# Where the normalised keys of a hybrid RWKV-7/GLA layer lie, and when their row sums are taken

## The chip, the cores and the metric

The kernel runs on one core of a Trainium2 chip. The metric is device time in microseconds (us) of one execution. A core has five engines with a queue of instructions each: TensorE (PE in the profile, with its weight loads as PEld), VectorE (DVE), ScalarE (ACT), GpSimd (POOL), and SyncE (SP), which here only issues DMAs. Each engine takes its queue strictly in order; between engines, instructions wait on semaphores.

## The reference

One layer of a decoder, for 1024 prompt tokens and 8 sequences of 4 sample tokens. What matters here is the RWKV-7 half of the mixing step (8 heads of 64 columns, so 512 columns each for r, k and v):

```python
xs = pa + (prev - pa) * mu                       # token shift of the projected columns
r, k, v, w_lo, a_lo, g_lo = split_cols(xs, [...])
decay = jnp.exp(-jnp.exp(w)); a = jax.nn.sigmoid(a0 + a_lo @ a_up)
kk = heads(k * k_k)
kk = kk * lax.rsqrt(jnp.maximum(jnp.sum(kk * kk, -1, keepdims=True), 1e-24))
k = k * (1.0 + (a - 1.0) * k_a)
# per token:  S = S*decay + (S @ -kk) (kk*a)^T + v k^T ;  o = S @ r
```

The second half of the mixing step is gated linear attention (GLA). Then come an output projection, a layer norm, a ConvGLU feed-forward of width 2816 and a second layer norm. The feed-forward is not touched.

## The kernel before

Everything is float32. Large products are taken in three passes over a high and a low part (`wh`, `wl` of the weights, `xh`, `xl` of the tokens), all accumulated in one PSUM bank.

The mixing step goes in two halves of tokens (H0: 512 prompt and 32 sample tokens, in two blocks of 272; H1: 512 prompt tokens, one block) and, within a half, in four pairs of heads. So there are eight pairs, numbered 0 to 7. `rwkv_prep` (L847) does one pair: with `shifted` (L766) it projects k, then r, then v, 128 columns each. One block of a projection is 24 matmuls into a bank of the PSUM pool `g`, which has two banks; then ACT evicts it and DVE adds the shifted rows, reading the same bank, so a bank comes free only after DVE's reads. `pair_rsqrt` (L288) normalises the keys: PE sums the squares `sq` over each head (`t<-sel,sq`, into the PSUM pool `t`, also two banks), DVE takes the inverse root by Newton steps on the small tile `rst` (L276 to L286), ACT spreads it over `sq` (L290), and PE transposes `sq` (`t<-ident,sq`, L75). From that DVE forms `kk` (L898), then `ar` (L910), POOL forms `ba` = kk times a (L908), and DVE forms `bk` from `ba` (L920). `post` (L938) needs `ar` and `bk` for its products `t<-ar,bk`.

Tiles with one tag share one place in SBUF and hold it one after the other. In `p2` the tag `e1` holds `sw`, then `sq`, then `ba`; the tag `e4` holds `kk` and then `v`. So the first write of `v` (ACT, L778) waits until the last reader of `kk` is done.

Five chains (chunk recurrence, inverse, tail and so on) and three streams (RWKV projections, GLA projections, output projection) are woven by a planner, `weave` (L187), which counts PE's time and steps a thread at each `yield`. The framework under it then sets the order in each engine's queue from its own estimate of when operands are ready, so the queues differ from the order of the text: orders shown below are those of the queues.

Of the kernel before, what the change touches and what calls it, by code (L numbers as in the profile page):

```python
# [9 lines left out]
F32 = mybir.dt.float32  # L10
# [7 lines left out]
P = 128  # L18
# [25 lines left out]
def step_kernel(  # L44
# [73 lines left out]
    def col(j):  # L118
        return vec[:, j:j + 1]
# [13 lines left out]
    p2 = cx.enter_context(tc.tile_pool(name="p2", bufs=1))  # L133
# [78 lines left out]
    def s1(shape, name, i):  # L212
        return rr_.tile(shape, F32, name=name, tag=f"s{i}")
# [6 lines left out]
    def win_tile(c0, m=P, raws=(None, None)):  # L220
        out = []
        for raw, k0 in zip(raws, (0, 4)):
            raw = raw or win_load(c0, k0, m)
            wh = px.tile([P, 4, m], F32R, name="wh", tag="wh", bufs=3)
            act.copy(wh, raw)  # L225
            wl = px.tile([P, 4, m], F32R, name="wl", tag="wl", bufs=3)
            pool.tensor_tensor(wl, raw, f(wh), ALU.subtract)  # L227
            out += [(wh[:, j, :], wl[:, j, :]) for j in range(4)]
        return out

    def gemm(ps, ws, s, e, m=P):
        for k in range(KT):
            wh, wl = ws[k]
            o = ps[:m, 0:e - s]
            pe.matmul(o, wh, xh[:, k, s:e], start=k == 0, stop=False)
            yield 0
            pe.matmul(o, wh, xl[:, k, s:e], start=False, stop=False)
            yield 0
            pe.matmul(o, wl, xh[:, k, s:e], start=False, stop=k == KT - 1)
            yield 0  # L240

    def gtile():
        return pg.tile([P, 512], F32, name="g", tag="g")
# [7 lines left out]
    def s3(ap):  # L251
        return ap.rearrange("p (b t) -> p b t", t=NS)
# [10 lines left out]
    def rows_rsqrt(cols, n, v0, v1, op0, op1):  # L263
        ps = ttile()
        for j in range((n + P - 1) // P):
            w = min(P, n - P * j)
            for sq, sel, c in cols:
                m = sel.shape[1]
                pe.matmul(ps[0:w, 32 * (2 * j + c):32 * (2 * j + c + m)], sq[:, P * j:P * j + w],
                          sel.unsqueeze(2).to_broadcast([P, m, 32]), start=True, stop=True)  # L270
        ps = ps.rearrange("p (x r) -> p x r", r=32)[:, :, 0]
        st = p1.tile([P, 3, 10], F32, name="rst", tag="rst", bufs=2)
        a, y, t = [st[:, i, 0:10 if n > 512 else 8] for i in range(3)]
        if n > 512:
            pool.memset(a[:, 8:10], 1.0)
            dve.tensor_scalar(a[0:32, 8:10], ps[0:32, 8:10], v0, v1, op0, op1)  # L276
        dve.tensor_scalar(a[:, 0:8], ps[:, 0:8], v0, v1, op0, op1)
        newton(a, y, t)
        return y
# [8 lines left out]
    def pair_rsqrt(sq, n, *ops):  # L288
        y = rows_rsqrt([(sq, sel2, 0)], n, *ops)
        act.copy(sq[:, 0:512].rearrange("p (a c) -> p a c", c=64), y[:, 0:8].unsqueeze(2).to_broadcast([P, 8, 64]))  # L290
        return y

    def pair_spread(ye):
        ps = ttile()
        for j in range(4):
            pe.transpose(ps[:, j * P:(j + 1) * P], ye[:, j * P:(j + 1) * P], ident)
        return ps
# [468 lines left out]
    def shifted(H, c0, xs, ws=None):  # L766
        ft = c0 // P
        ws = ws or win_tile(c0)
        mu, halo_ = col(V_MU + ft), halo[:, ft:ft + 1]

        def add_prev(out, prev):
            dve.scalar_tensor_tensor(out, prev, mu, out, ALU.mult, ALU.add)
        for s, e in H.blocks:
            ps = gtile()
            yield from gemm(ps, ws, s, e)
            ep = min(e, 512)
            m = ep - s
            act.activation(xs[:, s:e], ps[:, 0:e - s], AF.Identity, scale=omu[:, ft:ft + 1])  # L778
            add_prev(xs[:, s + 1:ep], ps[:, 0:m - 1])
            add_prev(xs[:, s:s + 1], halo_)  # L780
            dve.tensor_copy(halo_ if H.base + ep < NP else nsh[:, ft, 0:1], ps[:, m - 1:m])
            if e > 512:
                pv, xv = s3(ps[:, 512 - s:544 - s]), s3(xs[:, 512:544])
                add_prev(xv[:, :, 1:], pv[:, :, 0:NS - 1])
                add_prev(xv[:, :, 0], sst[:, ft, :])
                dve.tensor_copy(nsh[:, ft, 1:9], pv[:, :, NS - 1])
# [9 lines left out]
    def take(gen, n):  # L796
        for _, item in zip(range(n), gen):
            yield item
# [48 lines left out]
    def rwkv_prep(Q):  # L847
        H, p = Q.H, Q.p
        n, sam = H.n, H.sam
        pcs = Q.pcs = rr_.tile([P, 8], F32, name="pcs", tag="pcs", bufs=3)  # L850
        pc0 = p * P
        cs = slice(pc0, pc0 + P)
        sw = p2.tile([P, 544], F32, name="sw", tag="e1")
        aa = s1([P, 544], "aa", 0)
        k = s1([P, 544], "k", 2)
        main = shifted(H, 512 + pc0, k)
# [28 lines left out]
        sq = p2.tile([P, 544], F32, name="sq", tag="e1")  # L885
        act.activation(sq[:, 0:n], k[:, 0:n], AF.Square, scale=col(V_KK + p))
        rr = s1([P, 544], "r", 3)
        yield from shifted(H, pc0, rr)
        y = pair_rsqrt(sq, n, 1e-24, 0.0, ALU.max, ALU.add)
        if Q.i >= 2:  # L890
            yield ("wait", f"C{Q.i - 2}")
        Q.E = rr_.tile([P, 8, 2, 2, CH], F32, name="E", tag="E", bufs=2)
# [1 line left out]
        Q.bkT = rr_.tile([P, 8, P], F32, name="bkT", tag="bkT", bufs=2)  # L894
        Q.ar = ars[Q.i % 2]
        Q.bon = rr_.tile([P, 512], F32, name="bon", tag="bon", bufs=2)
        kk = p2.tile([P, 544], F32, name="kk", tag="e4")
        dve.scalar_tensor_tensor(kk[:, 0:512], k[:, 0:512], col(V_KK + p), pair_spread(sq), ALU.mult, ALU.mult)  # L898
        if sam:
            ps = ttile()  # L900
# [3 lines left out]
            dve.scalar_tensor_tensor(kk[:, 512:544], k[:, 512:544], col(V_KK + p), ps[:, 0:32], ALU.mult, ALU.mult)  # L904
        arp = Q.ar
        bk = rr_.tile([P, 8, 2, CH], F32, name="bk", tag="bk")
        ba = p2.tile([P, 544], F32, name="ba", tag="e1")
        pool.tensor_tensor(ba[:, 0:n], kk[:, 0:n], aa[:, 0:n], ALU.mult)  # L908
        for h in range(2):
            dve.scalar_tensor_tensor(arp[own[h], :, 0, 1 - h, :], c3(kk)[own[h]], -1.0, pp[own[h], :, 0:CH],  # L910
# [264 lines left out]
    for hf, (base, n, blocks) in enumerate(HALVES):  # L1175
        H = Half()
# [95 lines left out]
    def stream_r():  # L1272
        for hf, H in enumerate(Hs):
            if hf:
                yield ("wait", "G0")
                yield from load_x(H)
                yield ("done", "X1")
            yield ("wait", "lock")
            yield from half_start(H, *([] if hf else [ws0]))
            yield ("free", "lock")  # L1280
            if hf == 0:
                constants()
                yield ("done", "X0")
            for Q in Qs[4 * hf:4 * hf + 4]:
                yield ("prio", R_PRIO[Q.i])
                yield ("wait", "lock")
                yield from rwkv_prep(Q)
                yield ("free", "lock")
# [468 lines left out]
```

## Time and profile before

| what | value |
|---|---|
| three runs | 1653.04, 1675.87, 1679.36 us |
| median | 1675.87 us |
| profiled execution, its own time | 1657.51 us |
| its span, first to last instruction | 1655.8 us |
| busy: PE, DVE, ACT, POOL | 95%, 57%, 32%, 22% |
| mean granted PE clock | 0.974 |

Idle time of PE is small as a share, and it lies almost all in the mixing step, which is the first 690 us. The runs differ among themselves by 1.6%. A row of the timeline gives start, duration, engine, line, operation, tile written, tiles read, count and, in brackets, how long the engine stood idle before it and what ended that.

### The profile page before, as it was taken

The numbers are of one execution on the slowest core, as the hardware profiler recorded it, in microseconds if no ns is written. First come the engines' busy times: TensorE is split into PE (matmuls) and PEld (weight loads), VectorE is DVE, ScalarE is ACT, GpSimd is POOL, SyncE is SP. The second block draws the span as 40 slices with busy tenths as digits, with TensorE's granted clock in tenths as the row PEclk, the third lists the DMA queues.
The fourth block names the chain that finished last, engine by engine and source line by source line (L and its number), as shares of the span: only waits on it lengthen the run. The fifth ranks groups of instructions, "written<-read, shape, count | busy, mean of one in ns | idle before, by whom it ended". The sixth has DMA issues, their size and how long they took to land.

```text
span 1655.8 us, 28781 instructions
## 1 busy us (share of the span) xinstructions
PE 1570.6 (95%) x11728; PEld 1324.3 (80%) x11728; DVE 945.6 (57%) x2083; ACT 529.4 (32%) x986; POOL 358.7 (22%) x583
## 2 busy tenths in 40 slices
PE   7899889889999999998999999999999999999997
PEld 6788777766676667666878898898988889888996
DVE  4566567676787767536774444544445443454348
ACT  4453443435444435344223131221202212121222
POOL 5434424323444343331000000000000000000005
PEclk9999998989999989999999999999999999999999
DMA  4122122131211013232313020210202112021102
GB/s 140 47 65 65 39 65 71 34 85 33 59 39 46 27 46 103 79 105 87 100 43 102 26 64 27 64 52 27 64 25 65 45 34 64 14 77 43 48 27 106
DMA packets 138572, 97.36 MB, mean 59 GB/s; under 512 B 15963, under 2 KB 127003, under 8 KB 138440
## 3 DMA queue, kind: packets, MB, share of 16 engines
q1 hardware_dynamic: 138440, 95.52, 19.5%
q8 instruction: 92, 1.51, 0.4%
q14 instruction: 40, 0.33, 0.1%
HBM read 84.36 MB, written 11.15 MB: 58 GB/s over the span
## 4 chain that ended last, share of the span: by engine, by line
PE 60%; DVE 5%; issue 2%; ACT 1%; POOL 1%; DMA 1%; DVEq 0%; POOLq 0%; ACTq 0%
PE g L71 26%; PE t L71 18%; PE dn L71 13%; PE t L75 1%; PE opso L71 1%; PE sps L71 1%; PE opsog L71 1%; DVE st L1485 0%; PE up L71 0%; DVE rst L285 0%; DVE yt L1665 0%; DVE ya L1642 0%; DVE tm L327 0%; DVE yt L1666 0%; PE rp L71 0%
## 5 line engine op out<-in xcount | busy, mean ns | idle before, releaser
L71 PE MATMUL g<-xh,wh 128*128 128x272 f32 (+1 forms) x624 | 221.3, 355 | 9.5 <-DVE sg L1094 3.5
L71 PE MATMUL g<-xh,wl 128*128 128x272 f32 (+1 forms) x624 | 215.2, 345 | 3.2 <-POOL wl L227 3.2
L71 PE MATMUL g<-xl,wh 128*128 128x272 f32 (+1 forms) x624 | 216.2, 347 | 0.0
L1458 DVE TENSOR_TENSOR wlu<-wraw,whu 128x1024 fp32r<-128x1024 f32 x45 | 55.1, 1224 | 229.2 <-ACT whu L1453 220.2
L227 POOL TENSOR_TENSOR wl<-wraw,wh 128x512 fp32r<-128x512 f32 x104 | 136.3, 1313 | 168.8 <-ACT wh L225 154.2
L1607 POOL COPY ncv<-gp 128x2 f32<-128x2 f32 x22 | 20.6, 936 | 610.1 <-ACT gp L1599 610.1
L71 PEld LDWEIGHTS g<-xh,wh 128*128 128x128 f32 x624 | 122.0, 196 | 22.6 <-issue 7.0
L71 PEld LDWEIGHTS g<-xh,wl 128*128 128x128 f32 x624 | 122.2, 196 | 11.4 <-POOL wl L227 3.7
L71 PE MATMUL g<-xb,whu 128*128 128x288 f32 (+1 forms) x688 | 130.9, 288 | 0.0
L71 PE MATMUL t<-xb,whu 128*128 128x256 f32 (+1 forms) x688 | 130.5, 288 | 0.0
L71 PEld LDWEIGHTS g<-xl,wh 128*128 128x128 f32 x624 | 122.3, 196 | 9.0 <-issue 3.3
L71 PEld LDWEIGHTS t<-xb,whu 128*128 128x128 f32 x688 | 109.7, 189 | 1.8
L71 PEld LDWEIGHTS g<-xb,whu 128*128 128x128 f32 x688 | 109.7, 189 | 1.8
L71 PE MATMUL t<-xa,whu 128*128 128x512 f32 x352 | 110.2, 394 | 0.0
L225 ACT CAST wh<-wraw 128x512 fp32r<-128x512 f32 x104 | 64.0, 618 | 131.1 <-PE g L71 79.3
L71 PE MATMUL g<-xa,whu 128*128 128x512 f32 x336 | 105.6, 395 | 0.0
L1642 DVE TENSOR_TENSOR ya<-ya,dn 128x512 f32<-128x512 f32 x108 | 73.3, 684 | 53.7 <-PE dn L71 53.7
L71 PE MATMUL g<-xb,wlu 128*128 128x256 f32 (+1 forms) x344 | 99.3, 289 | 0.0
L71 PE MATMUL t<-xb,wlu 128*128 128x256 f32 (+1 forms) x344 | 99.2, 288 | 0.0
L71 PE MATMUL dn<-whd,hh 128*128 128x512 f32 x240 | 94.9, 395 | 0.0
L71 PE MATMUL dn<-wld,hh 128*128 128x512 f32 x240 | 94.6, 394 | 0.0
L71 PE MATMUL dn<-whd,hl 128*128 128x512 f32 x240 | 94.3, 393 | 0.0
(515 smaller groups left out, 3518.9 us busy)
## 6 DMA issues: line engine op xcount, KB each, us to landing
wraw<-in_w_in_dram SPq DMA_DIRECT2D x104, 256.0 KB
wraw<-in_w_up_dram SPq DMA_DIRECT2D x43, 512.0 KB
wraw<-in_w_down_dram SPq DMA_DIRECT2D x22, 512.0 KB
xt<-in_x_prompt_dram SPq DMA_DIRECT2D x16, 256.0 KB
woraw<-in_w_out_dram SPq DMA_DIRECT2D x7, 512.0 KB
ob<-od SPq DMA_DIRECT2D x7, 512.0 KB
out_dram<-yt SPq DMA_DIRECT2D x6, 512.0 KB
ya<-in_x_prompt_dram SPq DMA_DIRECT2D x5, 512.0 KB
```

Source lines behind the costliest of these rows:

```text
L71: return nc.tensor.matmul(out, lhsT, rhs, **kw)
L75: return nc.tensor.transpose(out, in_, idn)
L225: act.copy(wh, raw)
L227: pool.tensor_tensor(wl, raw, f(wh), ALU.subtract)
L1458: dve.tensor_tensor(wl, raw, f(wh), ALU.subtract)
L1607: pool.tensor_copy(ncv[:, i, 0:2], gp[:, 1024:1026])
L1642: dve.tensor_tensor(y[:, cs], y[:, cs], ps, ALU.add)
```

## The change

Two things. First, the places: `kk` now takes tag `e1`, the place of the squares, which it follows; `ba` no longer has a tile, and POOL writes kk times a over `aa`; `v` is alone in `e4`. Second, the row sums: r's projection is started, stopped at half of its matmuls (24 of 48 in H0, after the first block; 12 of 24 in H1), then `pair_rsqrt` is emitted, then the rest of r's projection.

```diff
         rr = s1([P, 544], "r", 3)
-        yield from shifted(H, pc0, rr)
+        main = shifted(H, pc0, rr)
+        yield from take(main, 24 if sam else 12)
         y = pair_rsqrt(sq, n, 1e-24, 0.0, ALU.max, ALU.add)
+        yield from main
         if Q.i >= 2:
             yield ("wait", f"C{Q.i - 2}")
...
-        kk = p2.tile([P, 544], F32, name="kk", tag="e4")
+        kk = p2.tile([P, 544], F32, name="kk", tag="e1")
...
-        ba = p2.tile([P, 544], F32, name="ba", tag="e1")
+        ba = aa
         pool.tensor_tensor(ba[:, 0:n], kk[:, 0:n], aa[:, 0:n], ALU.mult)
```

PE's queue in pair 0, at the row sums (`g_609` and `g_638` or `g_659` are r's two blocks, `g_735` is v's first). Before:

```order
L71 MATMUL g_638<-xh_112,wh_605 128x272
L71 MATMUL g_638<-xl_113,wh_605 128x272
L71 MATMUL g_638<-xh_112,wl_607 128x272
L71 MATMUL t_670<-sel2_71,sq_594 128x64 x4
L71 MATMUL t_670<-sel2_71,sq_594 32x64
L71 MATMUL g_735<-xh_112,wh_725 128x272
L71 MATMUL g_735<-xl_113,wh_725 128x272
L71 MATMUL g_735<-xh_112,wl_727 128x272
```

Now:

```order
L71 MATMUL g_609<-xh_112,wh_605 128x272
L71 MATMUL g_609<-xl_113,wh_605 128x272
L71 MATMUL g_609<-xh_112,wl_607 128x272
L71 MATMUL t_634<-sel2_71,sq_594 128x64 x4
L71 MATMUL t_634<-sel2_71,sq_594 32x64
L71 MATMUL g_659<-xh_112,wh_599 128x272
L71 MATMUL g_659<-xl_113,wh_599 128x272
L71 MATMUL g_659<-xh_112,wl_601 128x272
```

The sums stood between r and v; they stand now between r's two blocks, 24 matmuls earlier.

PE's queue in pair 0, at the transposes of `sq` (`g_764` is v's second block, `g_734` now v's first). Before:

```order
L71 MATMUL g_764<-xh_112,wl_733 128x272
L71 MATMUL g_764<-xh_112,wh_731 128x272
L75 MATMUL t_696<-ident_61,sq_594 128x128 x4
L71 MATMUL t_702<-ident_61,rst_676 64x32 x2
L71 MATMUL g_764<-xl_113,wh_731 128x272
L71 MATMUL g_764<-xh_112,wl_733 128x272
```

Now:

```order
L71 MATMUL g_734<-xh_112,wh_724 128x272
L71 MATMUL g_734<-xl_113,wh_724 128x272
L75 MATMUL t_696<-ident_61,sq_594 128x128 x4
L71 MATMUL t_702<-ident_61,rst_640 64x32 x2
L71 MATMUL g_734<-xh_112,wl_726 128x272
L71 MATMUL g_734<-xh_112,wh_724 128x272
```

They came after 40 of v's 48 matmuls, with 8 left behind them; they come after 2, with 46 left.

DVE's queue in pair 0, at the Newton steps (`rst`). Before:

```order
L276 TENSOR_SCALAR rst<-t 32x2
L277 TENSOR_SCALAR rst<-t 128x8
L917 TENSOR_TENSOR ar_299<-r,pp 64x8x64
L282 TENSOR_SCALAR rst<-rst 128x10
L925 TENSOR_TENSOR sar<-r,pps 128x32
L284 SCALAR_TENSOR_TENSOR rst<-rst 128x10
L934 SCALAR_TENSOR_TENSOR r<-r,vec,k_571 128x544
L285 TENSOR_TENSOR rst<-rst 128x10
L286 SCALAR_TENSOR_TENSOR rst<-rst 128x10
```

Now:

```order
L276 TENSOR_SCALAR rst<-t 32x2
L277 TENSOR_SCALAR rst<-t 128x8
L772 SCALAR_TENSOR_TENSOR r<-halo,vec,r 128x1
L282 TENSOR_SCALAR rst<-rst 128x10
L781 COPY halo<-g 128x1
L284 SCALAR_TENSOR_TENSOR rst<-rst 128x10
L285 TENSOR_TENSOR rst<-rst 128x10
L286 SCALAR_TENSOR_TENSOR rst<-rst 128x10
```

The three larger instructions on r that stood among the Newton steps now stand behind `kk` (L919, L927 and L936 there); two tiny ones take their place.

## Rows read from the trace of the kernel before

**Rows 1.** The page: busy time of each engine; PE's granted clock in 40 slices.

```profile
PE 1570.6 (95%) x11728; PEld 1324.3 (80%) x11728; DVE 945.6 (57%) x2083; ACT 529.4 (32%) x986; POOL 358.7 (22%) x583
PEclk9999998989999989999999999999999999999999
```

**Rows 2.** Windows of mixing and feed-forward: length, busy time by engine, clock, DMA, GB/s.

```profile
0.00:690.00 690.00, 623.14 (x6202) 504.07 (x6204) 461.14 (x1274) 299.08 (x569) 279.99 (x444) 0.94 0.22 62
690.00:1656.00 966.00, 947.43 (x5528) 820.20 (x5528) 484.49 (x809) 230.29 (x417) 78.72 (x139) 1.00 0.18 57
```

**Rows 3.** Timeline of pair 0, from r's first eviction to the transposes of sq.

```profile
46.68 0.49 ACT L778 ACTIVATE r<-g,omu 128x272 f32<-128x272 f32 x1 [1.03 <-PE g L71]
49.48 1.23 PE L71 MATMUL t<-sel,sq 128*128 128x64 f32 x10
50.64 0.39 PE L71 MATMUL g<-xh,wh 128*128 128x272 f32 x1
51.34 1.42 DVE L917 TENSOR_TENSOR ar<-r,pp 64x512 f32<-64x512 f32 x1
53.05 0.79 DVE L934 SCALAR_TENSOR_TENSOR r<-r,vec,k 128x544 f32<-128x544 f32 x1
55.46 0.62 ACT L290 COPY sq<-rst 128x512 f32<-128x512 f32 x1 [5.23 <-DVE rst L286]
55.65 0.28 PE L71 MATMUL g<-xh,wh 128*128 128x272 f32 x1
56.13 0.66 PE L75 MATMUL t<-ident,sq 128*128 128x128 f32 x4 [0.20 <-ACT sq L290]
```

**Rows 4.** Timeline of pair 0, from kk to the next projection (fwh).

```profile
56.82 0.75 DVE L898 SCALAR_TENSOR_TENSOR kk<-k,vec,t 128x512 f32<-128x512 f32 x1 [1.48 <-PE t L75]
57.81 1.71 POOL L908 TENSOR_TENSOR ba<-kk,aa 128x544 f32<-128x544 f32 x1 [1.13 <-DVE kk L904]
58.34 1.73 DVE L910 SCALAR_TENSOR_TENSOR ar<-kk,pp 64x512 f32<-64x512 f32 x1
61.16 1.38 DVE L920 TENSOR_TENSOR bk<-ba,cum 64x512 f32<-64x512 f32 x2
61.34 0.87 ACT L778 ACTIVATE v<-g,omu 128x272 f32<-128x272 f32 x2 [2.54 <-POOL pp L871]
62.68 0.49 DVE L772 SCALAR_TENSOR_TENSOR v<-g,vec,v 128x271 f32<-128x271 f32 x1
62.69 2.90 PE L71 MATMUL t<-ar,bk 128*128 128x256 f32 x6 [2.13 <-DVE bk L920]
65.02 0.79 PE L71 MATMUL g<-xh,fwh 128*32 128x272 f32 x1
```

**Rows 5.** Timeline of pairs 1, 2 and 3, PE behind the kk chain.

```profile
173.60 1.19 PE L71 MATMUL t<-ar,bk 128*128 128x256 f32 x2 [3.67 <-DVE gosb L695]
298.48 0.67 PE L71 MATMUL t<-ar,bk 128*128 128x256 f32 x2 [3.43 <-DVE gosb L695]
348.67 1.08 PE L75 MATMUL g<-ident,xt 128*128 128x128 f32 x4 [4.16 <-issue]
```

**Rows 6.** Timeline of pairs 4 and 5, PE.

```profile
438.26 0.43 PE L71 MATMUL up<-Rt,E 128*128 128x64 f32 x2 [2.29 <-DVE Rt L444]
476.16 1.10 PE L71 MATMUL t<-sel,sq 128*128 128x64 f32 x8
487.43 1.12 PE L75 MATMUL t<-ident,sq 128*128 128x128 f32 x4 [2.93 <-ACT sq L290]
```

**Rows 7.** Windows of the kk chain in pair 1, and behind the gaps of pairs 0, 1, 2.

```profile
158.40:175.40 17.00, 13.22 (x98) 11.81 (x98) 13.38 (x41) 3.73 (x7) 9.01 (x11) 0.94 0.33 94
62.00:66.00 4.00, 3.31 (x9) 2.49 (x10) 2.96 (x12) 0.20 (x1) 0.19 (x1) 0.50 0.25 66
174.00:178.00 4.00, 4.00 (x14) 3.01 (x14) 2.00 (x12) 0.00 (x0) 0.78 (x3) 0.65 0.24 86
299.00:303.00 4.00, 4.00 (x17) 3.58 (x16) 2.44 (x13) 0.00 (x0) 0.67 (x2) 0.58 0.20 74
```

## The prediction

> **What bounds the kernel now.** I read the page first, then windows by stage, then the timeline around each pair's keys. PE is busy 95% of the span and no other engine passes 57% [rows 1]: only time in which PE stands still, or runs at its lower clock, can be won. The windows say where that is [rows 2]. In the feed-forward PE is busy 947.43 of 966 us at a granted clock of 1.00. In the mixing step it is busy 623.14 of 690 us, idle for 66.9 us, at a mean clock of 0.94. [...] The change touches the mixing step alone.
>
> Pair 0 shows what stands still. Row sums run at 49.48, the spread copy of `sq` starts at 55.46, the transposes at 56.13 [rows 3]. `kk` follows at 56.82, `bk` ends at 61.16 + 1.38 = 62.54 [rows 4]. Meanwhile PE has run out: v's 48 matmuls take about 48 x 0.1285 = 6.2 us (first at 50.64, fortieth at 55.65, so 5.01 / 39 each [rows 3]) and end near 58. Both `g` banks then hold v, which ACT evicts only at 61.34, since `kk` has its place, and DVE reads from 62.68. The products `t<-ar,bk` begin at 62.69, the next projection (`fwh`) at 65.02 [rows 4]. So from 58 to 62.7 PE does almost nothing. The same shape follows in pairs 1, 2 and 3: single waits of 3.67, 3.43 and 4.16 us [rows 5]. In pairs 4 and 5 the waits are 2.29 and 2.93 us, and they end with DVE's chunk step and with the copy of `sq` [rows 6]. Behind these gaps the granted clock is 0.50, 0.65 and 0.58 in stretches of 4 us [rows 7].
>
> **The change, part by part.** Nothing is added or removed: the same matmuls, DVE, ACT and POOL instructions and DMAs. It moves them. SP's queue gets no new work; what follows on it is only earlier.
>
> *Row sums amid r, pair 0.* r's first block has been projected when its eviction starts at 46.68 [rows 3], so the sums run from there for 1.23 us, to 47.9, where before they began at 49.48. From the start of the sums to that of the copy it took 55.46 - 49.48 = 6.0 us, and in that stretch DVE also did 1.42 and 0.79 us of work on r [rows 3], which the queue now puts behind `kk`. Without them 3.8 us are left: the copy runs from 50.5 to 51.1. PE does r's second block (24 x 0.1285 = 3.1 us) and two matmuls of v, and arrives at 51.2. It hardly waits. `kk` then starts 0.7 us behind the transposes, as in rows 3 and 4, near 51.9, and some 1 us later where r's second eviction and its DVE reads go first. From `kk` to the end of `bk` took 62.54 - 56.82 = 5.7 us; the piece of `ar` now in between adds 0.7 (half of the 1.42, which ran beside POOL). `bk` ends near 59.3, against 62.54, 3.2 us earlier.
>
> *v's own place.* After the transposes 46 of v's matmuls are left, 46 x 0.1285 = 5.9 us of cover, which end near 58.1. ACT may evict v as soon as each block is done. But DVE's reads of those banks stand behind `bk` in its queue, so the banks come free near 60.5, not 58.5, and `fwh` starts there instead of 65.02: 4.5 us earlier. PE still waits about 1 us for `bk`. I take **4.0 us** for pair 0; the ends are 0 (DVE's queue holds all it held before) and 5 (no wait is left).
>
> *Pairs 1 to 3.* The same advance of 3.2 us meets waits of 3.67, 3.43 and 4.16 us [rows 5]. With a little lost to chunk steps in between I take 3.3 + 3.0 + 3.0 = **9.3 us**, between 0 and the 11.3 of the three waits.
>
> *Pairs 4 to 7.* Here a projection is one block, so the sums come half a projection earlier, but the waits that end with DVE's other work [rows 6] need not go. I take **2.5 us**, between 0 and 2.29 + 2.93 and as much again for pairs 6 and 7, 10 us.
>
> *The clock.* In the three stretches of rows 7 PE lost 4 x (0.50 + 0.35 + 0.42) = 5.1 us to the lower level, right behind a gap each time. The gaps shrink but don't all go: I take **3 us**, between 0 and 5.1. [...]
>
> *New waits.* ACT's copy of `sq` now stands ahead of r's second eviction and of the weight casts, so where DVE is late with the Newton steps, ACT's queue waits, and r's bank with it. Pair 5 shows how late: from sums at 476.16 to transposes at 487.43, 11.3 us, with 2.93 us of PE waiting [rows 6]; pair 0 shows 0.20 [rows 3]. Between 0.2 and 2.9 per pair I take 0.4, nearer to pair 0, since the queue places the transposes by an estimate that fitted there: 8 x 0.4 = **3 us** lost.
>
> *The places, otherwise.* `ba` over `aa` keeps `aa` until `bk` is read, and `kk` in `e1` keeps that place until `ar` is written. The next pair's first ACT writes come after v's projection, which is past `bk` in pair 0 by the times above. I cost both at nothing; if a projection did not cover them, the next pair's first evictions would wait by the length of the `ar` writes, up to 1.73 us [rows 4].
>
> Sum: 4.0 + 9.3 + 2.5 + 3 - 3 = 15.8, so 16 us less. The rest of the mixing step is bound by PE (90% busy) and is passed on whole, since the output projection follows the last pair. Against the profiled execution's own time of 1657.5 us that is 1641.5. The runs' median, 1675.87, lies 18.4 us above the profiled one, and the runs spread from 1653 to 1679; the new kernel's will spread alike. I take the middle of the two levels, (1657.5 + 1675.9) / 2 = 1666.7, less 16: **1650 us**.
>
> **The rivals.**
>
> *DVE is the bound, and nothing much is won* (chance 0.20). In the 17 us of pair 1's chain DVE is busy 13.38 us, 79% [rows 7]. If moving the Newton steps only shifts DVE's other work behind them, `bk` ends as late as now, and the banks wait for DVE in its queue order though `v` has a place. Against it: in pair 0 larger work on r leaves the stretch before `kk`. The gain is then 0 to 6 us: 1661 to 1667, say 1664. Rows 4 show one cause: the second write of `ar` took 1.73 us beside POOL's `ba`. [...]
>
> *The wait moves to the new sums, and it is slower* (0.10). If in each pair the copy of `sq` is as late as in pair 5, PE stands for 2.9 us at the transposes and ACT's queue stands with it: 8 x 2.9 = 23 us, of which 3.1 are there now (2.93 + 0.20). Left of the gains is at most the release of v's banks, about 7 us. Net +13 us: 1680. It decides where the time from the sums to the copy passes that of the PE work between them by more than some 2 us on average. For it: pair 5. Against it: pair 0's wait of 0.20.
>
> *All gaps and their clock go* (0.08). The 4.7 us of pair 0 from 58 to 62.7 with the waits of rows 5 and 6 make 4.7 + 11.3 + 5.2 = 21.2 us; with the clock's 5.1 and 6 us in pairs 6 and 7, 32 us: 1635.
>
> **How the numbers follow.** The forecast's case, a gain of 7 to 25 us, has 0.62. Its own range is 1642 to 1660 at the middle level, and the runs' levels lie 9 us to either side of that. The range of 1630 to 1672 takes in the forecast's case nearly whole, the case of nothing won except at the upper level's edge, and half of the last case; left out are the slower case and tails. What a measurement of this kernel can tell from no change is about 2%, 33 us: the runs alone spread by 1.6%. Faster by more than that needs the last case or the forecast's best with runs at the lower level: 0.12. Slower by more needs the slower case with runs at the upper level: 0.03. Within: 0.85.
>
> **What would show it.** In the profile after: row sums between r's two blocks, some 3 us before r's end; transposes of `sq` with waits under 1 us; the first `t<-ar,bk` of pairs 1 and 2 with a wait under 1 us, no longer over 3.4; v's eviction on ACT ahead of the end of `bk`; mixing step shorter by 14 to 18 us, its clock at 0.95, the feed-forward still 966 us. Wrong would be: waits at the transposes of 2 us and more in most pairs; `bk` no earlier behind r's projection than before; or gains in pairs 0 to 3 that pairs 4 to 7, whose queues also changed, give back.

## The result and the profile after

The changed kernel is slower, by little: 1672.47 us median of 20 runs against 1658.95 of 20 of the kernel before, a ratio of 1.0078 (95% interval 1.0060 to 1.0097), some 13 us. Forecast were 1650 us and a range of 1630 to 1672. Medians here are over all executions of a kernel; the ratios leave out those that took over 1.5% more than its fastest. The profiled execution took 1672.49 us, its span is 1670.7.

On the page PE is as busy as in [rows 1] (95%), but its granted clock has a hole in the seventeenth and eighteenth slice, near 670 to 740 us, that the page of before doesn't have:

```profile
PE 1587.5 (95%) x11728; PEld 1332.9 (80%) x11728; DVE 946.0 (57%) x2083; ACT 529.1 (32%) x986; POOL 357.0 (21%) x583
PEclk9999898999998999679999999999999999999999
```

To see where the 14.9 us of span went, both traces are cut at the same three events: the third, the seventh and the eighth tail (`t<-sel,sqo`, of pairs 2, 6 and 7). The row sums of pair 4 have passed the third: they stand just ahead of it now (408.47) and behind it before (428.68); as many matmuls of PE lie ahead of it as before, to within six. The eighth is the last one of the mixing step's recurrence. Windows of the kernel before (length, then PE busy, last but two the granted clock):

```profile
0.00:422.17 422.17, 375.62 (x3678) 319.73 (x3678) 265.59 (x735) 179.62 (x353) 167.60 (x276) 0.94 0.23 64
422.17:667.20 245.03, 228.33 (x2189) 169.54 (x2185) 182.34 (x512) 108.65 (x198) 105.72 (x160) 0.95 0.20 57
667.20:728.33 61.13, 56.92 (x604) 40.30 (x601) 26.80 (x68) 23.61 (x45) 21.81 (x35) 0.97 0.32 91
728.33:1655.80 927.47, 909.71 (x5268) 794.70 (x5267) 470.90 (x770) 217.48 (x393) 63.58 (x113) 1.00 0.17 55
```

And of the changed one:

```profile
0.00:410.65 410.65, 370.85 (x3684) 314.25 (x3684) 267.37 (x737) 180.12 (x353) 167.27 (x276) 0.96 0.25 66
410.65:660.68 250.03, 227.03 (x2180) 169.39 (x2174) 180.77 (x500) 107.32 (x194) 104.06 (x163) 0.94 0.20 55
660.68:740.53 79.85, 76.97 (x603) 53.11 (x602) 26.00 (x78) 24.91 (x47) 22.01 (x33) 0.70 0.27 73
740.53:1670.70 930.17, 912.70 (x5271) 796.12 (x5270) 471.87 (x771) 216.79 (x393) 63.62 (x113) 0.99 0.18 55
```

Read the lengths: 11.5 us won up to the third tail, 5.0 given back up to the seventh, 18.7 lost between the seventh and the eighth, 2.7 behind it. Over the whole run PE's idle time hardly changed (1655.8 - 1570.6 = 85.2 us, now 1670.7 - 1587.5 = 83.2); its busy time grew by 16.9 us, for the same number of matmuls. In the third stretch PE does the same some 600 instructions, is idle for less time than before (2.88 against 4.21 us), and runs at 0.70 of its clock. This stretch I call the seam.

**Pair 0** answers to [rows 3, 4]; the timeline after:

```profile
46.01 1.23 PE L71 MATMUL t<-sel,sq 128*128 128x64 f32 x10
51.80 0.62 ACT L290 COPY sq<-rst 128x512 f32<-128x512 f32 x1 [2.28 <-DVE rst L286]
52.47 0.66 PE L75 MATMUL t<-ident,sq 128*128 128x128 f32 x4 [1.78 <-ACT sq L290]
53.92 0.74 DVE L900 SCALAR_TENSOR_TENSOR kk<-k,vec,t 128x512 f32<-128x512 f32 x1
56.35 0.49 ACT L778 ACTIVATE v<-g,omu 128x272 f32<-128x272 f32 x1 [3.41 <-PE g L71]
57.98 1.41 DVE L922 TENSOR_TENSOR bk<-aa,cum 64x512 f32<-64x512 f32 x2
59.54 0.67 PE L71 MATMUL t<-ar,bk 128*128 128x256 f32 x2 [0.23 <-DVE bk L922]
62.16 0.29 PE L71 MATMUL g<-xh,fwh 128*32 128x272 f32 x1 [1.51 <-DVE halo L781]
```

The sums stand 3.5 us earlier, v is evicted ahead of `bk`, `bk` ends at 59.39 and `t<-ar,bk` hardly waits. The next projection starts at 62.16, not 65.02; it waits for DVE's reads of v's bank. Pairs 1 to 3 answer to [rows 5], and their own rows have no wait left; but in pair 1 a chunk step just ahead now waits for 2.70 us:

```profile
165.94 0.69 PE L71 MATMUL sps<-RU,bkT 128*128 128x64 f32 x2 [2.70 <-DVE RU L448]
167.21 1.05 PE L71 MATMUL t<-ar,bk 128*128 128x256 f32 x2
293.47 0.70 PE L71 MATMUL t<-ar,bk 128*128 128x256 f32 x2
347.40 0.59 PE L71 MATMUL t<-ar,bk 128*128 128x256 f32 x2
```

In pairs 4 to 6, against [rows 6], the transposes of pair 5 (465.33; its sums are at 458.69) wait no more for their copy, but the products behind the chunk steps and the tails do:

```profile
427.27 0.63 PE L75 MATMUL t<-ident,s0t 128*128 128x128 f32 x4 [2.80 <-DVE Rt L444]
465.33 0.66 PE L75 MATMUL t<-ident,sq 128*128 128x128 f32 x4
475.13 0.66 PE L75 MATMUL t<-ident,sqo 128*128 128x128 f32 x4 [3.59 <-ACT sqo L290]
```

**The seam.** PE's timeline in the changed kernel, around 690 us (`opsog<-s0t,ax` are the products of the second group of sample tokens, `up<-Rt,E` is a product of a chunk step, `g<-xh,wh` a piece of a projection):

```profile
673.38 0.20 PE L71 MATMUL t<-ty,x 32*32 32x16 f32 x1 [1.89 <-DVE gosb L695]
685.55 0.44 PE L71 MATMUL up<-Rt,E 128*128 128x64 f32 x2
685.92 0.56 PE L71 MATMUL opsog<-s0t,ax 64*64 64x64 f32 x6
688.09 1.15 PE L71 MATMUL opsog<-s0t,ax 64*64 64x64 f32 x18
689.98 0.68 PE L71 MATMUL opsog<-s0t,ax 64*64 64x64 f32 x8
693.05 1.11 PE L71 MATMUL opsog<-s0t,ax 64*64 64x64 f32 x8
696.08 0.79 PE L71 MATMUL g<-xh,wh 128*128 128x512 f32 x1
698.24 0.77 PE L71 MATMUL g<-xh,wl 128*128 128x512 f32 x1
```

Behind the wait of 1.89 us the granted clock was at its lower level once: 0.50 in every window of 2 us from 674 to 684, 0.95 in the next, and back at 1.00, the upper level, from 686 to 690. Eight sample products took 0.68 us at 689.98 and take 1.11 us at 693.05: with no wait in between (PE is busy for all of 686 to 694), the clock has gone down to 0.50 again. A window of it, where PE is busy for every one of 36 us at half its clock:

```profile
692.00:728.00 36.00, 36.00 (x146) 22.66 (x144) 7.75 (x25) 7.02 (x15) 8.09 (x13) 0.50 0.16 45
```

In the kernel before, the sample products at 689.93 are followed by a projection piece at 691.82, at full speed (0.50 us instead of 0.79; the granted clock is 1.00 from 686 to 696):

```profile
684.36 1.06 PE L71 MATMUL opsog<-s0t,ax 64*64 64x64 f32 x8
689.56 0.43 PE L71 MATMUL up<-Rt,E 128*128 128x64 f32 x2
689.93 1.15 PE L71 MATMUL opsog<-s0t,ax 64*64 64x64 f32 x18
691.82 0.50 PE L71 MATMUL g<-xh,wh 128*128 128x512 f32 x1
```

PE's queue has changed there. Before, 46 of the trace's 64 sample products and the last inverse steps stood ahead of pair 7's first chunk step (689.56); in the changed kernel that step (685.55) comes ahead of all sample products, the inverse steps have taken projection pieces with them, and from the start of the sample group to its last product (`t<-gxs,gw`) 24 projection products are left in place of 27. Which of these differences matters was not taken apart.

### The profile page after: what moved, and what is told of

The parts are those of the page before. It is cut to its first block, busy times and chain, and to the rows that moved or that the text cites. A ratio compares the mean times of both kernels' runs of the same rounds, so it can differ in the third digit from the quotient of the medians.

```text
span 1670.7 us, 28769 instructions
## 1 busy us (share of the span) xinstructions
PE 1587.5 (95%) x11728; PEld 1332.9 (80%) x11728; DVE 946.0 (57%) x2083; ACT 529.1 (32%) x986; POOL 357.0 (21%) x583
## 4 chain that ended last, share of the span: by engine, by line
PE 68%; DVE 8%; issue 2%; ACT 1%; POOL 1%; DMA 1%; DVEq 0%; ACTq 0%; POOLq 0%
PE g L71 29%; PE t L71 19%; PE dn L71 12%; PE t L75 2%; PE opso L71 1%; PE opsog L71 1%; PE up L71 1%; PE sps L71 1%; DVE tm L327 1%; PE rp L71 1%; DVE rst L285 0%; DVE bk L922 0%; DVE rst L284 0%; DVE st L1487 0%; DVE yt L1667 0%
## 5 line engine op out<-in xcount | busy, mean ns | idle before, releaser
L71 PE MATMUL g<-xh,wl 128*128 128x272 f32 (+1 forms) x624 | 219.4, 352 | 2.8 <-POOL wl L227 2.8
```

Of the source, the lines that this page charges most:

```text
L71: return nc.tensor.matmul(out, lhsT, rhs, **kw)
```

## The experiments

My theory after these traces, the *seam theory*: the pairs' gain is real, and the loss is one stretch of TensorE at its lower level, which pair 7's new order brings about. Its rivals: the new places cost a little in every pair (*places*), or the clock falls there by chance (*chance*). All ratios are to runs of the kernel before on the same chip, with 95% intervals.

**1. The change without pair 7** (`e5_not7`)

```diff
-        yield from take(main, 24 if sam else 12)
+        yield from take(main, (24 if sam else 12) if Q.i < 7 else 99)
...
-        kk = p2.tile([P, 544], F32, name="kk", tag="e1")
+        kk = p2.tile([P, 544], F32, name="kk", tag="e1" if Q.i < 7 else "e4")
...
-        ba = aa
+        ba = aa if Q.i < 7 else p2.tile([P, 544], F32, name="ba", tag="e1")
```

> The change for pairs 0 to 6 only; pair 7 keeps its row sums behind r and its places (kk in e4, ba in e1). TensorE's queue from pair 7 on is then the one of the kernel before, with the sample group's small products ahead of the last chunk steps. Seam theory (what is won in the pairs arrives, and all the loss comes from pair 7's new order, which lets TensorE fall to its lower level between 672 and 730 us): the 6.5 us that the last but one tail came earlier are kept and the 22 us at the lower level are not paid, so 1648 to 1654 us against 1659 before, no stretch of tens of us with a granted clock of 0.50 behind 670 us. Places theory (kk in e1 and ba over aa make the next pair wait, a little in every pair): most of the loss stays, 1665 to 1672. Chance theory (the clock falls there in some executions, whatever the queue): as the changed kernel, 1668 to 1674, with the low stretch.

Measured: 1651.47 us, ratio 0.9938 (0.9901 to 0.9975), faster than before. Leaving out one pair of eight turned the sign, as the seam theory said, and places is out. But the profiled execution was one of the longest of its twelve (1666.39 us), and it has the hole:

```profile
660.36:736.46 76.10, 72.72 (x604) 49.55 (x601) 26.88 (x68) 23.58 (x45) 21.69 (x35) 0.73 0.27 73
```

Each execution's mean granted clock is known: seven of the twelve took 1645 to 1652 us at 0.975 to 0.980, two took 1666 at 0.964; of the changed kernel's twenty none was above 0.968. So chance has a part: the same program falls in some executions and, judging by their mean clocks, not in others. That the queue sets how often is what the experiments from here on bear on.

**2. Pair 7 alone** (`e6_only7`; the same lines with `Q.i == 7`)

> The change for pair 7 only; pairs 0 to 6 as before. TensorE's queue from pair 7 on is then the one of the changed kernel: the inverse steps between projection matmuls, and the last pair's chunk steps inside the sample group. Seam theory: nothing won in the pairs, the loss at the seam paid in full, 1672 to 1682 us against 1659 before, with some 25 to 60 us at a granted clock of 0.5 to 0.7 between 675 and 740 us. Places theory: one pair of eight, 1658 to 1661. Chance theory: 1655 to 1675 with no tie to the queue.

Measured: 1675.01 us, ratio 1.0075 (1.0044 to 1.0106), with none of twelve above a mean clock of 0.968. Its seam:

```profile
666.86:744.99 78.13, 75.54 (x603) 52.18 (x602) 25.71 (x78) 24.92 (x47) 22.02 (x33) 0.72 0.27 74
```

The whole loss comes with pair 7, and no gain with it. This edit has both parts of the change in it; experiments 7 and 8 tell them apart.

**3. Dense products in the sample group** (`e4_fill`)

```diff
+    def fill(m):
+        ps = ttile()
+        for _ in range(m):
+            pe.matmul(ps, xh[:, 0, 0:P], xh[:, 0, 0:512], start=True, stop=True)
...
                     if b == 3:
+                        if g == 1:
+                            fill(3)
                         yield 0.0
```

> The changed kernel with twelve more dense products (128 x 128 x 512, no reader) on TensorE, in threes among the small products of the second sample group; their time at the upper level is 12 x 0.23 = 2.8 us. Seam theory in its form 'the clock falls again near 691 us because only small products stand there': the second fall goes and with it some 15 to 18 us of loss, 1655 to 1662 us against 1672 of the changed kernel. If the first fall near 674 us, behind the wait for the output tail, carries the rest with it whatever stands behind: 1670 to 1676. Places theory: 1673 to 1677.

**4. Small products in their place** (`e8_thin`)

```diff
-        for _ in range(m):
-            pe.matmul(ps, xh[:, 0, 0:P], xh[:, 0, 0:512], start=True, stop=True)
+        for _ in range(4 * m):
+            pe.matmul(ps[0:64, 0:64], ident[0:64, 0:64], ident[0:64, 0:64], start=True, stop=True)
```

> The control of the filled kernel: the changed kernel with 48 small products (64 x 64 x 64, no reader) at the same four places of the second sample group in place of the twelve dense ones, for about the same 3 us of TensorE's time. If dense products hold the clock: the low stretch behind 688 us stays, 1672 to 1678 us. If it was only the other order or the delay of 3 us that helped (the chunk steps run a little later): 1658 to 1664, as with the dense ones.

Measured: dense 1661.63 us, ratio 0.9977 (0.9943 to 1.0011), with one execution of 8336.40 us among the twelve, for a reason that no trace shows; small 1680.04 us, ratio 1.0104 (1.0073 to 1.0134), above the 1672 to 1678 expected. Their seams, dense first:

```profile
662.66:731.22 68.56, 64.86 (x615) 45.27 (x614) 26.25 (x78) 24.93 (x47) 22.03 (x33) 0.93 0.31 85
```

```profile
664.37:752.38 88.01, 84.70 (x699) 59.53 (x698) 26.06 (x78) 24.90 (x47) 21.97 (x33) 0.71 0.24 66
```

Work was added and 11 us came back; small work of the same place gave back nothing. The order at the seam is the same in both but for one pair of chunk products. The delay is not: each small product stands as two in the trace, 96 that follow each other some 0.06 us apart at the upper level, about 6 us against the 3.4 that the twelve dense ones take there (2.8 expected). So neither the order nor a delay brought the 11 us back, but the kind of product: large, dense ones. The dense kernel still falls once, behind the wait (0.50 from 678 to 686 us, 0.93 over the seam), as expected of the first fall, and not again behind it (1.00 from 688 to 704).

**5. and 6. The dense products without the loss to mend** (`e7_not7_fill`: experiments 1 and 3 together; `e9_before_fill`: experiment 3 on the kernel before)

> Pairs 0 to 6 changed, pair 7 as before, and the twelve dense products of 128 x 128 x 512 in the second sample group. The profiled execution of the kernel with pair 7 left alone took 1664.7 us of span with 17 us at the lower level from 684 to 720 us, while its median was 1651.5: the old order at the seam also falls at times. If a lack of dense products is what lets it fall: the low executions go, median 1646 to 1652, highest below 1660, in spite of 2.8 us more work. If the fall is decided by the wait ahead of the seam: median 1653 to 1656 (2.8 us more than 1651.5) and still some at 1666 to 1669.

> The kernel before with the same twelve dense products. Its runs spread from 1647 to 1675 us, and their mean granted clock from 0.976 to 0.960 with it. If that spread is the seam falling in some executions: the upper runs go, median 1653 to 1660 (1659 to 1663 without them), highest below 1668. If the spread has another place: 1661 to 1666, spread as it was.

Measured: 1659.30 us, 0.9995 (0.9966 to 1.0023); 1662.14 us, 1.0009 (0.9983 to 1.0034). Misses, both. Eleven of twelve runs of the first lie at 1654.5 to 1662.8 with clocks of 0.971 to 0.979, so the executions at 1666 are nearly gone (one of 1676 is left), but the median is 8 us above that of experiment 1, where the dense products added 3.3 us of work. The four tiles taken from the pool `t` and the new order may cost the rest; that wasn't tried. The second kept the spread of the kernel before, as the other case of its expectation had it: eleven executions lie at 1655.78 to 1668.44 us and one at 1689.30. Its profiled execution took 1662.23 us with the seam at full clock:

```profile
669.20:730.75 61.55, 55.97 (x610) 40.33 (x607) 27.16 (x68) 23.37 (x45) 21.62 (x35) 1.00 0.25 69
```

Where the seam falls seldom, filling it does not pay; where the spread that is left comes from is not shown.

**7. The row sums alone and 8. the places alone** (`e2_sums`, `e1_places`: the two parts of the diff, each by itself)

> The row sums amid r alone, in all pairs; kk in e4 with v, ba in e1, as before. The queue at the seam is as before. The places alone took 0.998 of the time before (0.995 to 1.002). If the sums carry the gain of the pairs: 1649 to 1656 us. If both are needed, because v still waits for kk's last reader: 1657 to 1662. If the sums lose without the places: above 1664.

> The places alone in all pairs (kk in e1, ba over aa, v alone in e4); row sums behind r as before. TensorE's queue at the seam is as before. Seam theory: no low stretch behind 670 us, and v's earlier eviction gives a part of the gain: 1652 to 1659 us. Places theory: the whole loss sits here, 1665 to 1675. If the sums carry all of the gain (v's eviction was covered anyway): 1657 to 1661.

Measured: sums 1667.77 us, 1.0027 (0.9999 to 1.0056), in the case of a loss by the time, though the interval still takes in no change; places 1660.09 us, 0.9984 (0.9946 to 1.0021). The expectation took the sums' queue at the seam for that of the kernel before. The trace shows another: product for product that of pair 7 alone, and that of the changed kernel but for the order among neighbouring 32 x 32 products, with the chunk step ahead of the sample products.

```profile
672.17 0.20 PE L71 MATMUL t<-ty,x 32*32 32x16 f32 x1 [1.60 <-DVE gosb L695]
680.10 0.43 PE L71 MATMUL up<-Rt,E 128*128 128x64 f32 x2
680.47 0.56 PE L71 MATMUL opsog<-s0t,ax 64*64 64x64 f32 x6
```

The places alone have the queue of the kernel before there. So it is pair 7's row sums that bring the new order, and the places have no part in it. All twelve runs of the sums have clocks of 0.962 to 0.967; of the 44 executions of the three kernels with the new order none has a mean clock above 0.968, while the places alone and the change without pair 7, with the old one, reach 0.979 and 0.980. Windows of the sums' seam, before the fall and in it:

```profile
672.00:684.00 12.00, 11.83 (x234) 9.20 (x234) 3.51 (x11) 5.01 (x13) 2.68 (x5) 1.00 0.27 85
686.00:722.00 36.00, 36.00 (x151) 22.66 (x149) 7.41 (x25) 7.02 (x15) 8.26 (x13) 0.50 0.16 44
```

PE had been busy for 11.83 of 12 us, its last longer wait (1.60 us) had ended at 672.17, and the clock was at its upper level; then it fell. But the order alone doesn't decide it, since with the old one the profiled execution of experiment 1 fell too (0.73). What else decides stays open.

**9. to 12. The sample group moved away from the seam** (`e10_early`: the whole change; `e11_before_early`: the kernel before; `e12_places_early`, `e13_sums_early`: the parts)

```diff
-                    if (1, 2)[q] == 2 * hf + g:
+                    if (1, 1)[q] == 2 * hf + g:
```

The second sample group now follows the first, where projection pieces stand among its products. (Where the expectations say sixth tail, it is the tail of pair 6, the seventh.)

> The changed kernel in full, with the second sample group moved: it comes right behind the first one (near 400 us) in place of near 680 us. No work is added or left out. In TensorE's queue behind the sixth tail there are then two to five projection products between any two small steps. Seam theory: no stretch of tens of us at 0.50 behind 670 us, the 19 to 22 us there come back, less what the later start of the second half's GLA costs: 1646 to 1656 us against 1672. If the low stretch only follows the sample group to 400 us: 1665 to 1675. If the loss of the changed kernel is not in the clock: 1668 or more.

> The kernel before with the same move of the second sample group: the base line for the three others of this call, without the seam. Seam theory: the upper runs of the kernel before (1665 to 1675) go, median 1650 to 1658. Difference of the changed kernel with the move to this one: what the change is worth in the pairs; from the sixth tail (667.2 to 660.7 us) 4 to 9 us are expected, against 16 of the prediction.

> The places alone, with the second sample group moved. With the seam out of the way: if the places are worth something of their own (v is evicted earlier), 3 to 6 us less than the kernel before with the same move; if v's banks wait for VectorE's queue anyway, the same within 2 us.

> The row sums amid r alone, with the second sample group moved. With the seam out of the way: if the sums carry the gain of the pairs, 4 to 9 us less than the kernel before with the same move, about equal to the whole change; if they need v's own place, the same within 2 us. The sums alone without the move took 1667.8 us, with the low stretch from 684 to 724 us: by the seam theory that was the seam and not the sums.

| with the sample group moved | executions | us | ratio to before | interval |
|---|---|---|---|---|
| kernel before | 12 | 1654.73 | 0.9996 | 0.9969 to 1.0022 |
| places alone | 7 | 1641.46 | 0.9905 | 0.9871 to 0.9939 |
| whole change | 6 | 1638.73 | 0.9872 | 0.9833 to 0.9910 |
| row sums alone | 6 | 1634.99 | 0.9860 | 0.9828 to 0.9891 |

The seams of the whole change and of the kernel before, each with the group moved:

```profile
668.92:727.55 58.63, 56.84 (x560) 42.97 (x559) 23.51 (x72) 25.20 (x43) 22.96 (x33) 0.91 0.30 91
```

```profile
690.98:747.71 56.73, 53.92 (x564) 41.05 (x561) 26.43 (x68) 24.69 (x42) 22.97 (x34) 0.97 0.30 90
```

And the stretch of the whole change to which the group has moved, at full clock:

```profile
440.00:460.00 20.00, 19.70 (x179) 15.74 (x177) 7.32 (x20) 6.31 (x15) 6.25 (x11) 1.00 0.22 58
```

This is the experiment that settles it: no work added or removed, the moved line alone does nothing to the kernel before, and the same change that costs 13 us now wins 1654.73 - 1638.73 = 16.0 us. It won more than the 4 to 9 I had expected of it. Between the profiled executions of the whole change, span times one less the mean clock fell from 1670.7 x 0.037 = 61.8 us to 1640.7 x 0.024 = 39.4, 22.4 of the 30.0 us between the spans. Against the moved kernel before the eighth tail comes 747.71 - 727.55 = 20.2 us earlier and some 8 us are given back behind it, where I have not followed them. The parts do not add up (13 for the places, 20 for the sums, 16 for both), and the intervals of the last two rows overlap: which part carries the gain is not told apart. Ten of the twelve runs of the moved kernel before lie within 1652.7 to 1655.8 us, a narrower spread than that of the kernel before; that the seam was its source is not shown, as filling the seam in experiment 6 did not narrow it. The row sums or the whole change with the group moved beat both given kernels.

## Why the prediction was wrong

- **"The rest of the mixing step is bound by PE (90% busy) and is passed on whole."** This is the step that failed. I had read the end of the mixing step as a place where PE works and time only shifts. But the row sums also moved pair 7's inverse and chunk steps, and the seam went from 61.13 us at 0.97 to 79.85 at 0.70: 18.7 us, more than the whole forecast gain. A busy share of 96% there (76.97 of 79.85) hid a clock of 0.50 over at least 36 us of it. The order of the queue at the seam shows the chunk steps slipping in among the sample products; the prediction looks at the pairs' keys only.
- *Row sums, pair 0*: right in mechanism. The copy and the transposes come 1.3 us later than forecast (51.80 and 52.47 against 50.5 and 51.2), `bk` ends at 59.39 (59.3 forecast): `kk` was late by 1 us and the way from `kk` to `bk` shorter by as much, which is luck. The wait at the transposes is 1.78 us, not under 1. The next projection gained 2.9 us of the 4.5, since DVE's reads of v's bank came later than I had put them.
- *Pairs 1 to 3*: the waits of the rows went, as forecast, but not the idle time behind them. Pairs 0 to 3 together gave 11.5 us up to the third tail, against 4.0 + 9.3 and a part of the clock's 3. Of these 6.75 are idle time of PE (46.55 became 39.80), half of the 13.3 forecast, as other steps wait instead (2.70 us for the chunk step in pair 1); the other 4.77 are busy time, shorter by the clock. That the total came near is luck. In pair 1 the clock took most of the gain: the products `t<-ar,bk` start 6.4 us earlier (167.21 against 173.60), the first tail only 1.2 (211.04 against 212.23), and the clock in the 20 us below costs 20 x (0.83 - 0.57) = 5.2 us more. Windows of 164 to 184 us, before and after:

```profile
164.00:184.00 20.00, 16.33 (x96) 13.96 (x96) 13.42 (x39) 6.16 (x10) 7.02 (x13) 0.83 0.14 41
```

```profile
164.00:184.00 20.00, 18.06 (x75) 14.65 (x76) 8.74 (x28) 4.67 (x7) 5.20 (x12) 0.57 0.11 27
```

  PE stands still for 1.94 us instead of 3.67, and runs at 0.57 instead of 0.83.
- *Pairs 4 to 7*: wrong in sign. 2.5 us were forecast, 5.0 were lost between the third and the seventh tail, where PE's idle time grew from 16.70 to 23.00 us. That pairs 4 to 7 give back what pairs 0 to 3 gain was one of the prediction's own signs of being wrong. PE's waits for the tails' copy of `sqo` grew from 5.3 to 8.2 us over the run, those of `sps<-RU`, a chunk step, from 0.8 to 7.9: taken from one chain, given to another.
- *The clock* (3 us back): mis-sized as a whole. By length times one less the clock, 422.17 x 0.06 = 25 us became 410.65 x 0.04 = 16 up to the third tail, better than forecast; the seam's 61.13 x 0.03 = 2 became 79.85 x 0.30 = 24.
- *New waits at the sums* (3 us): too dear; PE's waits for `sq` are 3.3 us in all, against 3.1. The slower rival, 1680 us, had nearly the right time with the wrong cause: PE does not wait at the sums; that its number came close is luck.
- *The base*: 1666.7 us was too high; twenty runs of the kernel before have a median of 1658.95. That hid 8 us of the miss: the measured 1672.47 lies half a us outside the range.
- *The feed-forward*: behind the eighth tail 927.47 became 930.17 us, nearly untouched as said.

## What to carry to other kernels

Where a change moves work in a queue, look at the order at every stage's end, not only where the change was meant to act: here a stretch of small products with fewer large ones between them cost 18.7 us, more than the three waits of [rows 5] together (11.3). Read the granted clock beside the busy share; 36.00 us busy of 36.00 at 0.50 is half a loss that the busy share calls full. And before a small gain is given up, move the place that ate it: one line turned 13 us slower into 20 us faster than before.

## What the runs showed of the hardware

TensorE's granted clock fell without the engine standing still: in the row sums alone it was busy for 11.83 of 12 us at 1.00 and then ran 36 us at 0.50, busy throughout; its last longer wait, of 1.60 us, had ended at the start of those 12 us. Small products (64 x 64 x 64, 128 x 128 x 64) stood in the queue where it fell; that they are the cause is the reading of experiments 3 and 4, and how they would act on the clock is not shown. With twelve products of 128 x 128 x 512 among them the clock was 1.00 from the first of these to 704 us in the three profiles that had them; with 48 of 64 x 64 x 64, which the trace shows as 96, it fell to 0.50 at 698 us, amid the sample group (over the whole seam of the changed kernel 0.93 with the dense ones, 0.71 with the small). One kernel (the change without pair 7) had mean clocks of 0.964 to 0.980 over twelve executions of 1645.14 to 1666.39 us; what differed between them is not shown.
